# The gated merge's sum and the last scaling of the rows leave VectorE for ScalarE and GpSimd; the queries' high half is cast on ScalarE

## The chip, the cores and the metric

The kernel runs on one core of a Trainium2 chip, from one launch. The metric is the device time of that launch in microseconds. Engines are called as the profile calls them: PE is TensorE (PEld its weight loads), DVE VectorE, ACT ScalarE, POOL GpSimd, and SP the queue that issues nearly all DMAs.

## The reference, cut to what matters

One decoder layer over 2048 rows of 1024 values: a combined projection, sparse attention (branch A), a chunked state-space scan (branch B), a gated merge of the two, an output projection, a residual, and a last RMSNorm. The change touches the parts below:

```
q, k = rope(q), rope(k);  o_a = softmax(top-256 keys) @ v * silu(z_a)
g_a, g_b = split(sigmoid(gates + gate_bias))
merged = g_a * (o_a @ w_branch_a) + g_b * (o_b @ w_branch_b)
x = x + merged @ w_out
out = x * rsqrt(mean(x*x) + eps) * final_norm_w
```

The kernel keeps fp32 accuracy with pairs of fp16 numbers: a value is split into a high half and the rest (low half), and a product takes three matmuls (high x high, high x low, low x high). The gates are stored as tanh(gate/2), so that a sigmoid is (tanh + 1) / 2.

## The kernel before, in words

The rows are worked in 16 tiles of 128. The first 1440 us are projections, the scan and the choice of keys. Then comes the stage that the change is in, to the end. Three streams are interleaved in it, by a rule that spends the estimated time of each in proportion:

- att_A(i) loads the queries of tile i (`q32`), splits them into fp16 halves `q1` (L1387, L1388), has them transposed by a DMA (`Q1`, L1393), and finds each row's largest logit: matmuls `lq` (L1401), each read by DVE (L1404). Its result goes into `q2`, and a second transposing DMA (`Q2`, L1419).
- att_B(i) goes over groups of 4 heads and 128 keys: two matmuls make logits `lg` (L1489, L1491), DVE adds the mask (L1498, tile `p32`), ACT takes the exponential (L1499) and casts it to fp16 `ph` (L1503), POOL makes the low half `pl` (L1506), and PE multiplies both with the values (L1434, L1435, L1444), three groups later. At the end of a tile POOL multiplies with the gate (L1450), and a DMA transposes the result (`oT`, L1351).
- fin_M(i) and fin_O(i) finish tile i in two halves of 512 columns. fin_M loads the gates (`gtl`, L1526, two buffers), makes `pa` (12 matmuls, L1530 to L1532) and `pb` (24, L1537 to L1539) in PSUM, and then on DVE: L1542 (gate + 1) x pa, L1543 (gate + 1) x pb, and L1544 the sum `mg` = first x `f1` + second, where `f1` (`va` in the profile) is one scale per row. ACT squares `mg` and sums it over the row (L1545). After both halves a row scale is made on DVE, ACT makes the fp16 high half (L1345), DVE the rest (L1348, tile `spm`), and a DMA transposes both into `mT` (L1351). fin_O multiplies `mT` with w_out (48 matmuls, L1568 to L1570), adds the residual on DVE (L1573, tile `xr`), squares it on ACT (L1574), makes 1/rms on DVE (L227 to L237), scales `xr` by it and by `final_norm_w` (L1580), and stores it (L1581).

PSUM has two buffers for `pa`, `pb` and fin_O's sums together, two for `lq` and two for `lg`. `p32` has three buffers, `mg`, `spm`, `mT` and `q1` one. fin_M(i+1) and fin_O(i) are interleaved, so that PE has work while the chain from `pb` to `mT` runs.

The order on each engine is not the order of the code: a scheduler with a cost model of its own puts the instructions of each engine into one fixed sequence. An engine runs its sequence in order, so an instruction that waits holds up all that stand behind it.

Of the kernel before, what the change touches and what calls it, by code (L numbers as in the profile page):

```python
# [15 lines left out]
AF = mybir.ActivationFunctionType  # L16
OP = mybir.AluOpType
# [7 lines left out]
NT = S // P  # L25
# [15 lines left out]
def MARK(label):  # L41
    pass
# [115 lines left out]
def hybrid_block(ctx, tc, a, out, dbg=None):  # L158
    nc = tc.nc
    V, A, PL, PE, SP = nc.vector, nc.scalar, nc.gpsimd, nc.tensor, nc.sync  # L160
# [1169 lines left out]
    def fips(shape):  # L1330
        return psF.tile(shape, FT, name="fi2", tag="fi2")
# [33 lines left out]
    def load_mt(i):  # L1365

        mts[i] = at.tile([P, NT, P], BF, name="mkt")
        SP.dma_start_transpose(mts[i][:, 0:i + 1], msk[i, :, 0:(i + 1) * P])

    def att_A(i):  # L1370

        MARK("attA")
        n = (i + 1) * P
        nck = (n + 511) // 512
        q32 = at.tile([P, H, HD], FT, name="q32")
        SP.dma_start(q32.rearrange("p h d -> p (h d)"), qd[i])
        mk = None
        if i >= 2:
            mk = at.tile([P, n if lag == 1 else S], BF, name="mka", bufs=1)
            SP.dma_start(mk[:, :n], msk[i, :, :n])  # L1380
            if lag > 1:
                load_mt(i)
        yield 1.0
        MARK("attA")
        q1 = at.tile([P, H, 2, HD], F16, name="q1", bufs=1)
        q2 = q2t[0]
        V.tensor_copy(q1[:, :, 0], q32)  # L1387
        V.tensor_tensor(q1[:, :, 1], q32, q1[:, :, 0], OP.subtract)  # L1388
        A.copy(q2[:, :, 0:64], q1[:, :, 0])
        yield 0.5  # L1390
        MARK("attA")
        Q1 = ac.tile([P, H, P], F16, name="Q1", bufs=2)
        SP.dma_start_transpose(Q1, q1.rearrange("p h a d -> p (h a d)"))  # L1393
        yield QY
        mxs_ = at.tile([P, H, 4], FT, name="mxs")
        for h in range(H):
            for c in range(nck):
                MARK("attA")
                c0, c1 = c * 512, min(n, c * 512 + 512)
                ps = psQ.tile([P, 512], FT, name="lq", tag="lq" if PQ_ else "lg2")  # L1400
                PE.matmul(ps[:, :c1 - c0], Q1[:, h], KHt[h // 4][:, c0:c1], start=True, stop=True)  # L1401
                jk = pw.tile([P, 512], BF, name="jk", tag="jk", bufs=1)
                if i >= 2:
                    V.tensor_tensor_reduce(jk[:, :c1 - c0], ps[:, :c1 - c0], mk[:, c0:c1], 1.0, -BIG, OP.add, OP.max, mxs_[:, h, c:c + 1])  # L1404
                else:
                    if i == 1:
                        V.tensor_reduce(mxs_[:, h, 1:2], ps[:, 0:P], axis=AX.X, op=OP.max)
                    V.tensor_tensor_reduce(jk[:, :P], ps[:, n - P:n], cmask, 1.0, -BIG, OP.add, OP.max, mxs_[:, h, 0:1])
                yield (c1 - c0) / 2400
        MARK("attA")  # L1410
        rm = at.tile([P, H], FT, name="rm")
        V.tensor_reduce(rm, mxs_[:, :, :(2 if i == 1 else nck)], axis=AX.X, op=OP.max)
        V.tensor_scalar(rm, rm, -(2.0 ** -15), None, OP.mult)
        V.tensor_copy(q2[:, :, 64], rm)
        V.tensor_tensor(q2[:, :, 65], rm, q2[:, :, 64], OP.subtract)
        yield 0.5
        MARK("attA")
        Q2 = ac.tile([P, H, P], F16, name="Q2", bufs=2)
        SP.dma_start_transpose(Q2, q2.rearrange("p h n -> p (h n)"))  # L1419
        st_[i] = (Q1, Q2)  # L1420
        yield 0.5
# [92 lines left out]
    def fin_M(i, fi):  # L1514
        rows = slice(i * P, (i + 1) * P)
        oT, f1 = oTs.pop(i)
        MARK("finM")
        obt = fi.tile([P, 2, KC, P], F16, name="obt", bufs=1)
        SP.dma_start_transpose(obt.rearrange("p a k t -> p (a k) t"), obn[i].rearrange("t a d -> t (a d)"))
        mg = fi.tile([P, D], FT, name="mg", bufs=1)  # L1520
        f2 = fi.tile([P, 2], FT, name="f2m")
        t = fi.tile([P, 2, D], F16, name="spm", bufs=1)
        for nh in range(2):
            cs_ = slice(512 * nh, 512 * nh + 512)
            gt = fi.tile([P, 2, 512], FT, name="gtl")
            SP.dma_start(gt, gd[i].rearrange("p (b n) -> p b n", b=2)[:, :, 512 * nh:512 * nh + 512])  # L1526
            pa = fips([P, 512])
            for k in range(4):
                MARK("finM")
                PE.matmul(pa, oT[:, 0, k], wpa[0][:, k, cs_], start=(k == 0), stop=False)  # L1530
                PE.matmul(pa, oT[:, 0, k], wpa[1][:, k, cs_], start=False, stop=False)
                PE.matmul(pa, oT[:, 1, k], wpa[0][:, k, cs_], start=False, stop=(k == 3))  # L1532
                yield 0.64
            pb = fips([P, 512])
            for k in range(KC):
                MARK("finM")
                PE.matmul(pb, obt[:, 0, k], wpb[0][:, k, cs_], start=(k == 0), stop=False)  # L1537
                PE.matmul(pb, obt[:, 0, k], wpb[1][:, k, cs_], start=False, stop=False)  # L1538
                PE.matmul(pb, obt[:, 1, k], wpb[0][:, k, cs_], start=False, stop=(k == KC - 1))  # L1539
                yield 0.64  # L1540
            MARK("finM")
            V.scalar_tensor_tensor(gt[:, 0], gt[:, 0], 1.0, pa, OP.add, OP.mult)  # L1542
            V.scalar_tensor_tensor(gt[:, 1], gt[:, 1], 1.0, pb, OP.add, OP.mult)  # L1543
            V.scalar_tensor_tensor(mg[:, cs_], gt[:, 0], f1, gt[:, 1], OP.mult, OP.add)  # L1544
            A.activation(t[:, 1, cs_].bitcast(BF), mg[:, cs_], AF.Square, accum_out=f2[:, nh:nh + 1])  # L1545
        V.tensor_tensor(f2[:, 0:1], f2[:, 0:1], f2[:, 1:2], OP.add)
        s_m, v_m = rowscale(f2[:, 0:1], "rm", fi)
        fo = fi.tile([P, 1], FT, name="fo")
        V.tensor_tensor(fo, v_m, io, OP.mult)
        mT = fi.tile([P, 2, KC, P], F16, name="mT", bufs=1)  # L1550
        yield from split_T(mg, s_m, t, mT, KC, i == NT - 1)
        st_[-1 - i] = (mT, fo)

    def fin_O(i, fi):
# [3 lines left out]
        xr = [fi.tile([P, 512], FT, name="xr", bufs=3) for _ in range(2)]  # L1558
# [4 lines left out]
        for nh in range(2):  # L1563
            cs_ = slice(512 * nh, 512 * nh + 512)
# [12 lines left out]
        rs = rsqrt_h(s1[:, 0:1], "fr", fi)  # L1577
        for nh in range(2):
            cs_ = slice(512 * nh, 512 * nh + 512)
            V.scalar_tensor_tensor(xr[nh], xr[nh], rs, fnw[:, cs_], OP.mult, OP.mult)  # L1580
            SP.dma_start(out[rows, cs_], xr[nh])  # L1581
        yield 0.1

# [43 lines left out]
    def early_att():  # L1627
        for i in range(NA):
            yield from att_A(i)
            yield from att_B(i)  # L1630
            flush()
        yield from att_A(NA)
# [13 lines left out]
    fnw = wf.tile([P, D], FT, name="fnw")  # L1646
# [121 lines left out]
```

## Time and profile before

| what | us |
|---|---|
| median of three runs (lowest, highest) | 2208.75 (2206.44, 2212.06) |
| the profiled execution: time / span of its instructions | 2205.71 / 2204.0 |
| PE busy over the span | 2034.3 (92%) |
| DVE busy | 1762.2 (80%) |
| ACT busy | 1131.5 (51%) |
| POOL busy | 833.1 (38%) |
| mean granted clock of PE | 0.974 |

Busy times overlap. PE's busy time comes from modelled ends of pipelined matmuls, so matmuls overlap in it and a wait is a little longer than the idle time shown. A wait is put down to the engine whose event came last.

### The profile page before, as it was taken

The numbers are of one execution on the slowest core, as the hardware profiler recorded it, in microseconds if no ns is written. First come the engines' busy times: TensorE is split into PE (matmuls) and PEld (weight loads), VectorE is DVE, ScalarE is ACT, GpSimd is POOL, SyncE is SP. The second block draws the span as 40 slices with busy tenths as digits, with TensorE's granted clock in tenths as the row PEclk, the third lists the DMA queues.
The fourth block names the chain that finished last, engine by engine and source line by source line (L and its number), as shares of the span: only waits on it lengthen the run. The fifth ranks groups of instructions, "written<-read, shape, count | busy, mean of one in ns | idle before, by whom it ended". The sixth has DMA issues, their size and how long they took to land. (4 is left out here: it accounts for less than half of the span.)

```text
span 2204.0 us, 45401 instructions
## 1 busy us (share of the span) xinstructions
PE 2034.3 (92%) x16625; PEld 1394.0 (63%) x16625; DVE 1762.2 (80%) x4798; ACT 1131.5 (51%) x1973; POOL 833.1 (38%) x1176
## 2 busy tenths in 40 slices
PE   6898999899999999989999899888999999999987
PEld 4656666566767878868877788644444545545543
DVE  8888888888888577888998887467878888887763
ACT  5444453434343167547745731245566666666671
POOL 4433334543435533311102125124454444445550
PEclk9999999999999999999999999999999999999998
DMA  5444422332223332442344435385455343334231
GB/s 155 122 114 108 97 69 81 96 88 63 66 62 89 102 91 80 89 125 90 119 140 132 130 109 180 93 236 124 103 124 112 99 112 93 78 91 97 72 82 46
DMA packets 371202, 229.19 MB, mean 104 GB/s; under 512 B 209996, under 2 KB 333720, under 8 KB 370968
## 3 DMA queue, kind: packets, MB, share of 16 engines
q1 hardware_dynamic: 370968, 226.19, 38.2%
q8 instruction: 132, 2.16, 0.4%
q14 instruction: 102, 0.84, 0.1%
HBM read 123.82 MB, written 53.90 MB: 81 GB/s over the span
## 5 line engine op out<-in xcount | busy, mean ns | idle before, releaser
L1506 POOL TENSOR_TENSOR pl<-p,ph 128x512 f16<-128x512 f32 x272 | 324.9, 1197 | 427.5 <-ACT ph L1503 426.8
L1499 ACT ACTIVATE p<-p,lnb,qsc 128x512 f32<-128x512 f32 x270 | 217.8, 811 | 216.6 <-DVE p L1498 215.7
L444 PEld LDWEIGHTS <-xh 128*128 128x128 f16 x2560 | 252.5, 100 | 50.1 <-DMA xh<-th 10.7
L445 PEld LDWEIGHTS <-xh 128*128 128x128 f16 x2560 | 251.3, 99 | 38.4 <-issue 3.2
L446 PEld LDWEIGHTS <-xl 128*128 128x128 f16 x2560 | 251.0, 99 | 34.5 <-issue 3.3
L1498 DVE TENSOR_TENSOR p<-lg,mkt 128x512 f32<-128x512 f32 x266 | 181.7, 685 | 68.7 <-PE lg L1491 61.0
L1404 DVE CUSTOM_DVE_ANT_0 jk<-lq,mka 128x512 bf16<-128x512 f32 (+3 forms) x304 | 187.9, 618 | 33.0 <-PE lq L1401 24.4
L1503 ACT CAST ph<-p 128x512 f16<-128x512 f32 x272 | 166.1, 615 | 6.5
L1090 ACT ACTIVATE jkS<-sca,XX 128x384 int8<-128x384 f32 (+3 forms) x104 | 138.6, 1333 | 54.0 <-DVE XX L1080 35.3
L1401 PE MATMUL lq<-KK,Q 128*128 128x512 f16 (+3 forms) x320 | 100.1, 347 | 19.2 <-DVE mxs L1404 14.3
L1491 PE MATMUL lg<-Q,KK 128*128 128x512 f16 x272 | 103.2, 382 | 12.1 <-DMA Q<-q2t 12.0
L1092 DVE TENSOR_SCALAR_CACHE_REDUCE jkV<-sca,XX 128x1536 uint8<-128x1536 f32 (+4 forms) x78 | 111.9, 1434 | 2.6
L1568 PE MATMUL fi<-wo,mT 128*128 128x512 f16 x256 | 98.5, 385 | 15.8 <-DMA mT<-spm 11.1
L1169 ACT ACTIVATE gt<-gt 128x512 f32<-128x512 f32 x64 | 40.1, 627 | 139.8 <-DVE gt L1168 139.4
L1434 PE MATMUL po<-Vt,ph 128*128 128x65 f16 x1088 | 106.4, 193 | 2.4 <-ACT ph L1503 2.1
L954 ACT ACTIVATE r<-acc 128x512 f32<-128x512 f32 (+3 forms) x152 | 79.6, 542 | 55.7 <-DVE sca L955 37.3
L1489 PE MATMUL lg<-Q,KK 128*128 128x512 f16 x272 | 103.8, 382 | 4.0 <-DVE p L1498 3.9
L1435 PE MATMUL po<-Vt,ph 128*128 128x64 f16 x1088 | 106.9, 195 | 0.0
L1444 PEld LDWEIGHTS <-pl 128*128 128x128 f16 x1088 | 65.2, 98 | 57.7 <-issue 5.7
L738 ACT ACTIVATE sj<-zu 128x256 bf16<-128x256 f32 x64 | 26.6, 415 | 145.6 <-POOL zu L736 145.6
L1537 PE MATMUL fi<-wpb,obt 128*128 128x512 f16 x256 | 97.3, 380 | 3.1 <-DVE gtl L1542 2.8
L1569 PE MATMUL fi<-wo,mT 128*128 128x512 f16 x256 | 98.1, 383 | 0.0
(804 smaller groups left out, 6648.1 us busy)
## 6 DMA issues: line engine op xcount, KB each, us to landing
bc<-acr SPq DMA_DIRECT2D x64, 256.0 KB, 3.2
gd<-gt SPq DMA_DIRECT2D x64, 256.0 KB, 2.5
gtl<-gd SPq DMA_DIRECT2D x32, 512.0 KB, 4.0
xt<-in_x SPq DMA_DIRECT2D x16, 512.0 KB, 4.3
e<-ecr SPq DMA_DIRECT2D x128, 64.0 KB, 3.1
obn<-ohl SPq DMA_DIRECT2D x64, 128.0 KB, 2.2
pst<-in_w_out SPq DMA_DIRECT2D x16, 512.0 KB, 4.4
xr<-in_x SPq DMA_DIRECT2D x32, 256.0 KB, 3.1
```

The costliest lines, as they stand in the source:

```text
L444: PE.matmul(ps, xh[:, c, tk], hi[:, c], start=(first and c == 0), stop=False)
L445: PE.matmul(ps, xh[:, c, tk], lo[:, c], start=False, stop=False)
L446: PE.matmul(ps, xl[:, c, tk], hi[:, c], start=False, stop=(last and c == KC - 1))
L1090: A.activation(jkA[:, :n], sct[i], AF.Sign, bias=thr[:, 0, k:k + 1], scale=-1.0, accum_out=cnt[:, 0, k:k + 1])
L1092: V.tensor_scalar(jkV[:, :n], sct[i], thr[:, 0, k:k + 1], 0.0, OP.is_lt, OP.add, accum_out=cnt[:, 0, k:k + 1])
L1404: V.tensor_tensor_reduce(jk[:, :c1 - c0], ps[:, :c1 - c0], mk[:, c0:c1], 1.0, -BIG, OP.add, OP.max, mxs_[:, h, c:c + 1])
L1434: PE.matmul(B["po"][:, h, 0:65], ph[:, h], Vt[:, j, g, 0:65], start=(j == 0 and h == 0), stop=False)
L1435: PE.matmul(B["po"][:, h, 0:64], ph[:, h], Vt[:, j, g, 65:129], start=False, stop=False)
L1498: V.tensor_tensor(p32, ps, mb, OP.add)
L1499: A.activation(p32, p32 if masked and not onP else ps, AF.Exp, bias=lnb, scale=qsc[g])
L1503: A.copy(ph, p32)
L1506: PL.tensor_tensor(pl, p32, ph, OP.subtract)
```

## The change

Four edits, all in the last stage. The code of the last tile (i = 15) keeps the old form of the second, third and fourth.

1. The cast of the queries to their high half goes from DVE to ACT.
2. After the gate's load, ACT makes (gate A + 1) x f1 in place (an activation Identity with a per-row scale and bias), so that DVE's first product is a plain one.
3. The sum `mg` goes from DVE to POOL, as an addition of two fp32 tiles in SBUF.
4. The last scaling goes from one DVE instruction to two: ACT multiplies by the row's 1/rms, POOL by `final_norm_w`.

```
-        V.tensor_copy(q1[:, :, 0], q32)
+        A.copy(q1[:, :, 0], q32)
...
             SP.dma_start(gt, gd[i].rearrange("p (b n) -> p b n", b=2)[:, :, 512 * nh:512 * nh + 512])
+            if i < NT - 1:
+                A.activation(gt[:, 0], gt[:, 0], AF.Identity, bias=f1, scale=f1)
...
-            V.scalar_tensor_tensor(gt[:, 0], gt[:, 0], 1.0, pa, OP.add, OP.mult)
-            V.scalar_tensor_tensor(gt[:, 1], gt[:, 1], 1.0, pb, OP.add, OP.mult)
-            V.scalar_tensor_tensor(mg[:, cs_], gt[:, 0], f1, gt[:, 1], OP.mult, OP.add)
+            if i < NT - 1:
+                V.tensor_tensor(gt[:, 0], gt[:, 0], pa, OP.mult)
+                V.scalar_tensor_tensor(gt[:, 1], gt[:, 1], 1.0, pb, OP.add, OP.mult)
+                PL.tensor_tensor(mg[:, cs_], gt[:, 0], gt[:, 1], OP.add)
+            else:
+                V.scalar_tensor_tensor(gt[:, 0], gt[:, 0], 1.0, pa, OP.add, OP.mult)
+                V.scalar_tensor_tensor(gt[:, 1], gt[:, 1], 1.0, pb, OP.add, OP.mult)
+                V.scalar_tensor_tensor(mg[:, cs_], gt[:, 0], f1, gt[:, 1], OP.mult, OP.add)
...
-            V.scalar_tensor_tensor(xr[nh], xr[nh], rs, fnw[:, cs_], OP.mult, OP.mult)
+            if i < NT - 1:
+                A.activation(xr[nh], xr[nh], AF.Copy, scale=rs)
+                PL.tensor_tensor(xr[nh], xr[nh], fnw[:, cs_], OP.mult)
+            else:
+                V.scalar_tensor_tensor(xr[nh], xr[nh], rs, fnw[:, cs_], OP.mult, OP.mult)
             SP.dma_start(out[rows, cs_], xr[nh])
```

The scheduler makes new sequences from it. In what the kernel runs on these inputs, PE has the same instructions, and of its 31,449 rows most keep their order; SP's DMAs change places in seven spots. Lines after L1526 have other numbers in the changed kernel: L1528 is the new activation, L1546 the product with `pb`, L1547 POOL's sum, L1552 the square, L1589 POOL's scaling.

DVE at the second half of tile 6's merge, before:

```order
L1498 TENSOR_TENSOR p_22862<-lg_22859,mkt 128x512
L1387 CAST q_23840<-q_23728 128x8x64
L1388 TENSOR_TENSOR q_23840<-q_23728,q_23840 128x8x64
L1543 SCALAR_TENSOR_TENSOR gtl<-gtl,fi_22723 128x512
L1544 SCALAR_TENSOR_TENSOR mg<-gtl,va 128x512
L1498 TENSOR_TENSOR p_22899<-lg_22896,mkt 128x512
L1498 TENSOR_TENSOR p_22938<-lg_22935,mkt 128x512
L1546 TENSOR_TENSOR f2m<-f2m 128x1
```

And DVE at the same place in the changed kernel:

```order
L1498 TENSOR_TENSOR p_22886<-lg_22883,mkt 128x512
L1388 TENSOR_TENSOR q_23871<-q_23756,q_23871 128x8x64
L1546 SCALAR_TENSOR_TENSOR gtl<-gtl,fi_22747 128x512
L1498 TENSOR_TENSOR p_22923<-lg_22920,mkt 128x512
L1553 TENSOR_TENSOR f2m<-f2m 128x1
L1498 TENSOR_TENSOR p_22962<-lg_22959,mkt 128x512
L1338 TENSOR_SCALAR rmt<-f2m 128x1
```

The cast and the sum are gone from between the mask additions, and the sum over the row (`f2m`), which needs ACT's square, stands one mask addition earlier.

POOL near there before (`oa` is the attention's output of the tile):

```order
L1506 TENSOR_TENSOR pl<-p_22831,ph 128x512
L1506 TENSOR_TENSOR pl<-p_22862,ph 128x512
L1450 TENSOR_TENSOR oa<-oa,za 128x256
L1506 TENSOR_TENSOR pl<-p_22899,ph 128x512
L1506 TENSOR_TENSOR pl<-p_22938,ph 128x512
```

And POOL there in the changed kernel, up to the scaling of the tile before:

```order
L1506 TENSOR_TENSOR pl<-p_22886,ph 128x512
L1547 TENSOR_TENSOR mg<-gtl 128x512
L1506 TENSOR_TENSOR pl<-p_22923,ph 128x512
L1450 TENSOR_TENSOR oa<-oa,za 128x256
L1506 TENSOR_TENSOR pl<-p_22962,ph 128x512
L1506 TENSOR_TENSOR pl<-p_23016,ph 128x512
L1506 TENSOR_TENSOR pl<-p_23045,ph 128x512
L1506 TENSOR_TENSOR pl<-p_23108,ph 128x512
L1506 TENSOR_TENSOR pl<-p_23140,ph 128x512
L1589 TENSOR_TENSOR xr<-xr,fnw 128x512 x2
L1506 TENSOR_TENSOR pl<-p_23187,ph 128x512
```

The sum stands right behind the `pl` of the last group whose cast ACT has issued before it squares the sum; both scalings of a tile stand together between two `pl`.

ACT at this place before (`spm,f2m` is the square with its sum, L1545):

```order
L1499 ACTIVATE p_22862<-p_22862,lnb,qsc_9034 128x512
L1503 CAST ph<-p_22862 128x512
L1545 ACTIVATE spm,f2m<-mg 128x512
L1499 ACTIVATE p_22899<-p_22899,lnb,qsc_9034 128x512
L1499 ACTIVATE p_22938<-p_22938,lnb,qsc_9034 128x512
L1503 CAST ph<-p_22899 128x512
L1345 ACTIVATE spm<-mg,rms 128x1024
```

And ACT there in the changed kernel:

```order
L1387 CAST q_23871<-q_23756 128x8x64
L1499 ACTIVATE p_22886<-p_22886,lnb,qsc_9034 128x512
L1503 CAST ph<-p_22886 128x512
L1552 ACTIVATE spm,f2m<-mg 128x512
L1499 ACTIVATE p_22923<-p_22923,lnb,qsc_9034 128x512
L1503 CAST ph<-p_22923 128x512
L1345 ACTIVATE spm<-mg,rms 128x1024
```

The square (L1552) follows the cast `ph<-p_22886`, whose `pl` POOL does ahead of the sum: nothing else of ACT lies between them.

## Rows read from the trace of the kernel before

**Rows 1.** Stretch view: us, busy us of each engine (instructions), PE clock, DMA share, GB/s.

```profile
1450.00:2150.00 700.00, 651.26 (x5652) 343.88 (x5651) 563.83 (x1435) 437.39 (x702) 329.64 (x289) 0.99 0.43 105
```

**Rows 2.** Waits, 1450 to 2150 us: who for whom, us in total, times, longest.

```profile
ACT spm L1545 <- DVE mg L1544: 18.5, 11, 7.3
...
PE lq L1401 <- DVE mxs L1404: 13.2, 21, 1.5
...
PE fi L1568 <- DMA mT<-spm: 11.1, 6, 2.5
PE lg L1491 <- DMA Q<-q2t: 8.8, 5, 2.6
...
PE lg L1489 <- DVE p L1498: 3.9, 5, 1.3
PE fi L1568 <- DVE gtl L1542: 3.6, 2, 2.7
...
PE fi L1537 <- DVE gtl L1542: 2.8, 1, 2.8
```

**Rows 3.** Groups, DVE, 1450 to 2150 us: count | busy us, mean ns | idle before.

```profile
L1348 DVE SCALAR_TENSOR_TENSOR spm<-mg,rms,spm 128x512 f16<-128x512 f32 x30 | 32.7, 1128 | 5.7 <-ACT spm L1345 5.7
L1580 DVE SCALAR_TENSOR_TENSOR xr<-xr,fry,fnw 128x512 f32<-128x512 f32 x27 | 27.0, 1038 | 0.1
L1544 DVE SCALAR_TENSOR_TENSOR mg<-gtl,va 128x512 f32<-128x512 f32 x29 | 25.4, 875 | 0.2
...
L1387 DVE CAST q<-q 128x512 f16<-128x512 f32 x12 | 7.4, 616 | 8.6 <-DMA Q<-q 5.0 <-DMA q<-qd 2.6 <-ACT p L1499 0.9
```

**Rows 4.** Groups, POOL and ACT, the same stretch.

```profile
L1506 POOL TENSOR_TENSOR pl<-p,ph 128x512 f16<-128x512 f32 x262 | 313.0, 1197 | 352.7 <-ACT ph L1503 352.2
L1499 ACT ACTIVATE p<-p,lnb,qsc 128x512 f32<-128x512 f32 x261 | 210.7, 811 | 204.3 <-DVE p L1498 203.4
...
L1503 ACT CAST ph<-p 128x512 f16<-128x512 f32 x261 | 159.5, 615 | 6.4
...
L1450 POOL TENSOR_TENSOR oa<-oa,za 128x256 f32<-128x256 f32 x27 | 20.3, 752 | 18.6 <-DVE oa L1449 15.9 <-DVE rms L1339 2.4
...
L1345 ACT ACTIVATE spa<-oa,ras 128x512 f16<-128x512 f32 x13 | 9.3, 712 | 0.6 <-DVE ras L1339 0.6
```

**Rows 5.** Timeline, DVE near 1614 us: start, us, engine, line.

```profile
1613.00 1.41 DVE L1580 SCALAR_TENSOR_TENSOR xr<-xr,fry,fnw 128x512 f32<-128x512 f32 x2
...
1615.06 0.69 DVE L1404 CUSTOM_DVE_ANT_0 jk<-lq,mka 128x512 bf16<-128x512 f32 x1
```

**Rows 6.** Timeline, PE at the same time.

```profile
1613.68 0.38 PE L1401 MATMUL lq<-KK,Q 128*128 128x512 f16 x1
1613.90 0.38 PE L1489 MATMUL lg<-Q,KK 128*128 128x512 f16 x1
1615.81 0.22 PE L1401 MATMUL lq<-KK,Q 128*128 128x128 f16 x1 [1.53 <-DVE mxs L1404]
```

**Rows 7.** Tile mg: shortest/median/longest duration in ns.

```profile
L1544 DVE SCALAR_TENSOR_TENSOR mg<-gtl,va x32: 722/751/1609, 1440.8 to 2175.7; 128x512 f32<-128x512 f32 x32
...
L1348 DVE SCALAR_TENSOR_TENSOR spm<-mg,rms,spm x32: 735/766/1655, 1460.1 to 2179.7; 128x512 f16<-128x512 f32 x32
```

**Rows 8.** Timeline, DVE and POOL near 1774 us.

```profile
1773.69 1.16 POOL L1506 TENSOR_TENSOR pl<-p,ph 128x512 f16<-128x512 f32 x1 [2.02 <-ACT ph L1503]
...
1773.79 1.61 DVE L1544 SCALAR_TENSOR_TENSOR mg<-gtl,va 128x512 f32<-128x512 f32 x1
```

**Rows 9.** Timeline, DVE, ACT and POOL at the merge of tile 6, second half.

```profile
1744.88 1.16 POOL L1506 TENSOR_TENSOR pl<-p,ph 128x512 f16<-128x512 f32 x1 [0.92 <-ACT ph L1503]
...
1745.60 0.99 DVE L1544 SCALAR_TENSOR_TENSOR mg<-gtl,va 128x512 f32<-128x512 f32 x1
...
1746.62 0.63 ACT L1545 ACTIVATE spm<-mg 128x512 bf16<-128x512 f32 x1 [1.88 <-DVE mg L1544]
```

**Rows 10.** Tile gtl: the load's time from issue to landing.

```profile
DMA to landing us min/median/max: 3.9/4.0/5.7
```

## Prediction

> **What bounds the kernel now.** I read the stretch view first, for the only stage that the change touches: of the 700 us from 1450 to 2150, DVE is busy 563.8 (81%), ACT 437.4 (62%), POOL 329.6 (47%), and PE shows 651.3 at a granted clock of 0.99 [rows 1]. PE is the engine that sets the pace, with DVE close behind it. So I asked the waits next, for what PE itself waits for [rows 2]. Two sorts matter. DVE ends 13.2 + 3.9 + 3.6 + 2.8 = 23.5 us of PE's idle time in 29 waits, most of them of the `lq` matmul, whose two PSUM buffers DVE must read first. Transposing DMAs end 11.1 + 8.8 = 19.9 us in 11 waits, `mT` and `Q2`. The idle time understates a wait: at 1613.90 PE issues a matmul, at 1615.81 the next, 1.91 us where matmuls follow each other by 0.22 us (1613.68 to 1613.90), so 1.69 us are lost where the row says 1.53 [rows 6]. With 0.16 us more for each wait, DVE costs PE 23.5 + 29 x 0.16 = 28.1 us, and the DMAs 19.9 + 11 x 0.16 = 21.7 us. Nothing that the change does can win more than part of these 50 us; the rest of the stage is matmuls.
>
> Why DVE is late can be seen at that same wait: the two scalings of L1580 held DVE for 1.41 us from 1613.00, and only at 1615.06 did it come to the `lq` result for which PE was waiting [rows 5]. DVE is fast enough on average; it is late after bursts, and the sums, the scalings and the fp16 remainders make the bursts.
>
> **DVE: what is removed.** In this stage 27 of L1580, 29 of L1544 and 12 of L1387 are shown [rows 3], and all of them go (the last tile's keep their place, but run after 2150). That is 27.0 + 25.4 + 7.4 = 59.8 us, so DVE falls from 563.8 to about 504 us, 72%. The first product loses its added constant and keeps its length. What of the 59.8 reaches PE is bounded by 0 (the bursts that remain suffice for every wait) and by all 28.1 us. I take half, 14 us: about a quarter of DVE's bursts goes, and the time that DVE needs to work off a burst shrinks faster than its load, since its idle share grows from 19% to 28%. Nothing is gained from the wait ahead of L1387 (8.6 us, mostly for DMAs [rows 3]): L1388 now waits at the same place for ACT's cast, which waits for the same DMAs.
>
> **ACT: what is added.** 30 activations with a per-row scale and bias, at L1499's 811 ns (it has both); 30 scaled copies, at L1345's 712 ns; 12 casts, at L1503's 615 ns [rows 4]: 24.3 + 21.4 + 7.4 = 53.1 us, which makes ACT 490 us, 70%. This lies beside ACT's idle time, most of which is waiting for DVE's mask additions (203.4 us [rows 4]). The new activation also waits for the gates' load. That load is issued when POOL's sum has freed the buffer, which is when ACT may start the square, and lands 4.0 us later [rows 10]. In the first halves of the later tiles one or two exponentials stand between, so ACT gets there after some 0.8 + 0.8 + 0.6 = 2.2 us and is held up to 1.8 us. Behind it wait the exponentials, for which PE has three groups of cover. I take 1 us for it all; 0 to 6 would be the bounds (15 waits of 1.8 us are 27 us of ACT, of which I let a fifth through).
>
> **POOL: what is added.** 30 sums and 30 products of 128 x 512 fp32 values with both inputs in SBUF. The nearest row has 1197 ns for this size with an fp16 output; 752 ns for half the size in fp32 bounds it from above with 1504 [rows 4]. At 1197 it is 71.8 us, and POOL goes to 401 us, 57%. POOL's own idle time covers that (it waits 352.2 us for `ph` [rows 4]). What it costs lies in two other places.
>
> The first is the path from `pb` to `mT`, on which the sum lies. A sum takes 1197 ns in place of DVE's mean of 875, 0.3 us more, and stands behind one `pl`. In tile 6 POOL is busy with that until 1744.88 + 1.16 = 1746.04; a sum would then end at 1747.24 and the square start 0.6 us later than its 1746.62 [rows 9]. Against that, where DVE had other work between the second product and the sum, POOL is earlier, and the chain's later steps on DVE find it less busy. I take 0.4 us for each chain; PE waited for `mT` 6 times by its matmuls, some 8 tiles have no slack to speak of, so 8 x 0.4 = 3 us. Bounds: 4 us won (0.5 us earlier each) and 15 x 1.5 = 22 us lost.
>
> The second is that DVE and POOL block each other. L1544 usually takes 751 ns, but 1609 at 1773.79, just after POOL began a `pl` of 1.16 us [rows 7, 8]; L1348 has a mean of 1128 and a shortest of 735, so 30 x 0.39 = 11.8 us of its time are waiting [rows 3, 7]. With POOL busy 57% in place of 47% that becomes a fifth more, 2.5 us of DVE time; priced like the removed work (14 / 59.8) it is 0.6 us. The removed instructions were blocked too, and their means include it. The Trainium skill (SBUF — State Buffer, "Who interferes with whom") gives this as a rule: an instruction of VectorE with two SBUF inputs and one of GpSimd that reads SBUF share a port pair, and the one that starts second is blocked for the whole of the other. By that rule, the trace agrees: the longest L1544 is its shortest plus 0.89 us, most of a `pl`. It speaks against giving GpSimd more to do, and with every one of the 30 L1348 blocked for a whole `pl` DVE would lose 30 x (1.2 - 0.39) = 24 us more, which at the same price changes the sum by 5.7 us.
>
> SP is held longer by the output rows, which now wait for ACT's copies and POOL's products (about 0.7 x 2 + 1.2 x 2 = 3.8 us in place of 1.4). Behind them in its queue stand the loads of the next `xr`, whose buffers they free, and then a gate load that has to wait for the next sum anyway; I cost it at nothing, and up to 2 us a tile where `Q2` or `oT` stands close behind.
>
> **The sum.** -14 + 1 + 3 + 0.6 = -9.4 us. On the profiled execution (2205.7) that is 2196.3. The median of the runs is 3.0 us above that execution, so the median should come to 2199.
>
> **Rivals.** *The waits change hands.* PE gains on `lq` and arrives sooner at `mT` and `Q2`, whose transposes take as long as before. For: 21.7 us of PE's waits are for DMAs already, and the tiles that wait for `mT` have no slack, so what PE wins between `pb` and `mT` it loses there. Against: the DVE waits are spread over the tile, and that path is perhaps a third of it; `Q2` also depends on DVE's maxima, which come sooner. It would leave some 4 us: about 2205.
>
> *GpSimd's queue is the new late one; slower.* The sum waits behind a `pl`, which waits for ACT's cast, and ACT has nothing to do between that cast and the square. If the chain to `mT` is 1.5 us longer in each of the 15 tiles, it is 22 us; the scalings, two together, 2.4 us, hold back `pl` and the product before `oT` as well, which DVE's next row scale waits for. With 3 us for that and 14 us won on DVE the kernel is some 11 us slower, about 2220. It decides from about 0.9 us per tile on. For: ACT already lost 18.5 us waiting for the sum [rows 2]. Against: tile 6 shows 0.6 us, and POOL stands idle more than half of the time.
>
> *DVE's waits go altogether.* With all 28.1 us gone and the costs above (28 - 4.6 = 23.5 us), 2185. For: at 72% a queue is seldom long. Against: L1348's pairs, often over 2 us, stay.
>
> That the change is without effect can be left out: the order of the instructions shows what has moved.
>
> **How the numbers follow.** Chances: the forecast 0.50 (its own range 2190 to 2202), DVE's waits gone 0.10, hands changed 0.24, GpSimd late 0.16. About 0.3% (6.6 us) is what a measurement of this kernel can tell from no change. Forecast and third rival are faster by more than that: 0.60; the first rival is within it: 0.24; the second is slower: 0.16. The range from 2186 to 2216 leaves out a little of the best and of the worst case.
>
> **What the profile after would show.** In the corresponding 700 us DVE is busy about 505 us; `lq`'s waits for DVE fall from 13.2 to 5 to 8 us; POOL's sums and products take about 1.2 us; ACT's wait for the sum, now POOL's, is no longer than 25 us; PE's waits for `mT` are 11 to 16 us. I am wrong if PE's waits for DVE stay near 23 us (the bursts that remain are the cause), or if the waits for `mT` or for `ph` grow by as much as DVE's shrink.

## The result, and the profile after

The changed kernel takes 2224.32 us (median of 6 runs, 2221.59 to 2230.59) where the kernel before takes 2209.99 (6 runs on the same chip, 2206.01 to 2212.06). The ratio is 1.0074, with a 95% interval of 1.0058 to 1.0089: slower by 0.74%, some 16 us on 2210. (Ratios are estimated from the single runs, so they are not quite the quotients of the medians, which lie 14.3 us apart here.) The forecast was 2199 us and faster; 2224 lies outside its range.

The profiled execution of after took 2230.59 us, the longest of its six, and its first sum `mg` already starts 6.8 us later than that of before (1447.6 against 1440.8 [rows 7]), in a part of the program that the change hardly touches (three of edit 1's sixteen casts lie there); over all the profiles below that start varies from 1440.8 to 1453.4. So I compare the stage alone, from the first start of an instruction that makes `mg` to the last. In before that is 1440.8 to 2175.7, 734.9 us [rows 7]. In after it is 1447.6 to 2199.5, 751.9 us, in the rows of the tile `mg` (shortest/median/longest duration in ns, first and last start):

```profile
L1547 POOL TENSOR_TENSOR mg<-gtl x30: 1270/1297/1732, 1447.6 to 2162.2; 128x512 f32<-128x512 f32 x30
...
L1551 DVE SCALAR_TENSOR_TENSOR mg<-gtl,va x2: 752/752/752, 2191.7 to 2199.5; 128x512 f32<-128x512 f32 x2
```

The stage is 17.0 us longer, which is the whole loss by the ratio. The stretch view of the stage, before and then after (columns as in [rows 1]), shows in what form:

```profile
1440.80:2175.70 734.90, 684.17 (x5834) 359.51 (x5833) 576.17 (x1454) 447.22 (x721) 337.98 (x294) 0.99 0.43 105
1447.60:2199.50 751.90, 687.93 (x5834) 360.45 (x5833) 521.13 (x1384) 488.38 (x791) 404.58 (x352) 0.98 0.43 103
```

PE has the same 5834 matmuls in both. Its busy time grew by 3.8 us, at a mean granted clock of 0.98 where it was 0.99. Its idle time, the rest of the stage, grew by 13.2 us, from 50.7 to 64.0. So the lower clock can account for no more than these 3.8 us of the 17.0; the rest is waiting.

The same view for 700 us of after, beside [rows 1], shows that the relief of DVE itself came as worked out:

```profile
1450.00:2150.00 700.00, 640.61 (x5476) 336.09 (x5475) 501.58 (x1340) 463.89 (x750) 384.79 (x336) 0.98 0.44 106
```

DVE went from 563.8 to 501.6 us. But in the same 700 us PE finished 5476 matmuls where it had finished 5652 [rows 1]. The waits of after, 1450 to 2175 us (who for whom, us in total, times, longest), say who was late:

```profile
ACT spm L1552 <- POOL mg L1547: 51.7, 26, 3.2
...
ACT gtl L1528 <- DMA gtl<-gd: 24.3, 16, 3.5
DVE f2m L1553 <- ACT spm L1552: 21.0, 14, 2.8
PE lq L1401 <- DVE mxs L1404: 17.3, 17, 2.1
DVE q L1388 <- ACT q L1387: 16.6, 8, 4.6
...
PE lg L1491 <- DMA Q<-q2t: 10.4, 7, 2.8
PE fi L1575 <- DVE gtl L1545: 9.8, 5, 3.3
...
PE fi L1575 <- DMA mT<-spm: 7.3, 3, 3.3
...
PE po L1434 <- ACT ph L1503: 4.6, 7, 1.0
PE fi L1539 <- DVE gtl L1545: 4.5, 2, 3.8
...
PE lg L1489 <- DVE rmt L1338: 3.0, 4, 1.4
```

PE's four largest waits for DVE are 17.3 + 9.8 + 4.5 + 3.0 = 34.6 us, where they were 23.5 [rows 2], although DVE has less to do. The rows of DVE and ACT above them say why: DVE stands still for 21.0 us at the f2 sum, because ACT's square is not done, and for 16.6 us at L1388, because ACT's cast is not done. ACT in turn stands still for 51.7 us at the square, because GpSimd's sum is not done; in before that wait was 18.5 us and for DVE [rows 2]. PE's waits for DMAs are no larger: 10.4 + 7.3 = 17.7 us against 19.9.

One case in full, from the timeline of after near 1770 us (start, us, engine, line; in brackets the idle time before and what ended it):

```profile
1767.78 0.62 ACT L1503 CAST ph<-p 128x512 f16<-128x512 f32 x1
...
1768.28 0.69 DVE L1498 TENSOR_TENSOR p<-lg,mkt 128x512 f32<-128x512 f32 x1
...
1768.54 1.17 POOL L1506 TENSOR_TENSOR pl<-p,ph 128x512 f16<-128x512 f32 x1 [1.61 <-ACT ph L1503]
...
1769.66 1.28 POOL L1547 TENSOR_TENSOR mg<-gtl 128x512 f32<-128x512 f32 x1
...
1770.97 0.63 ACT L1552 ACTIVATE spm<-mg 128x512 bf16<-128x512 f32 x1 [2.57 <-POOL mg L1547]
...
1771.60 0.80 ACT L1499 ACTIVATE p<-p,lnb,qsc 128x512 f32<-128x512 f32 x1
...
1771.73 0.16 DVE L1553 TENSOR_TENSOR f2m<-f2m 128x1 f32<-128x1 f32 x1 [2.75 <-ACT spm L1552]
1771.81 0.69 DVE L1498 TENSOR_TENSOR p<-lg,mkt 128x512 f32<-128x512 f32 x1
1771.83 0.38 PE L1577 MATMUL fi<-wo,mT 128*128 128x512 f16 x1
...
1772.43 0.62 ACT L1503 CAST ph<-p 128x512 f16<-128x512 f32 x1
...
1772.55 0.38 PE L1489 MATMUL lg<-Q,KK 128*128 128x512 f16 x1 [0.35 <-DVE rmt L1338]
...
1773.19 1.16 POOL L1506 TENSOR_TENSOR pl<-p,ph 128x512 f16<-128x512 f32 x1 [2.25 <-ACT ph L1503]
```

The sum waits in GpSimd's queue for a `pl`, which waits for ACT's `ph`. ACT, next in its own queue, has the square and stands for 2.57 us; DVE, next in its queue, has the f2 sum and stands for 2.75 us. Behind the square stands the exponential of the next group, although DVE had finished its mask addition at 1768.97; behind the f2 sum stands the mask addition of 1771.81. That addition ends at 1772.50 and gives PE its `lg` bank back, so the `lg` matmul starts at 1772.55 (the row names `rmt`, which DVE runs next), 0.72 us after the matmul before it where 0.22 is usual. And GpSimd, whose sum had started all this, then stands idle for 2.25 us, since ACT's cast is late. Three engines wait in a ring for one instruction of 1.28 us.

### The profile page after: what moved, and what is told of

It reads as the page before. It is cut to its first block, busy times and chain, and to the rows that moved or that the text cites. A ratio compares the mean times of both kernels' runs of the same rounds, so it can differ in the third digit from the quotient of the medians.

```text
span 2228.9 us, 45543 instructions
## 1 busy us (share of the span) xinstructions
PE 2041.1 (92%) x16625; PEld 1397.2 (63%) x16625; DVE 1705.7 (77%) x4722; ACT 1176.8 (53%) x2049; POOL 900.9 (40%) x1236
## 4 chain that ended last, share of the span: by engine, by line
PE 44%; DVE 25%; DMA 9%; issue 8%; ACT 8%; POOL 6%; SPq 1%; DVEq 0%; POOLq 0%; ACTq 0%
PE acc L444 5%; PE acc L446 5%; PE acc L445 5%; DVE cac L551 3%; PE lq L1401 2%; DVE bc L701 2%; PE fi L1539 2%; PE fi L1540 2%; PE fi L1541 2%; PE lg L1491 2%; PE lg L1489 2%; PE fi L1575 2%; PE fi L1577 2%; PE fi L1576 2%; DMA Q<-q2t 1%
## 5 line engine op out<-in xcount | busy, mean ns | idle before, releaser
L1506 POOL TENSOR_TENSOR pl<-p,ph 128x512 f16<-128x512 f32 x272 | 318.5, 1176 | 343.0 <-ACT ph L1503 342.7
L446 PEld LDWEIGHTS <-xl 128*128 128x128 f16 x2560 | 250.9, 99 | 34.6 <-issue 3.9
L1575 PE MATMUL fi<-wo,mT 128*128 128x512 f16 x256 | 98.2, 384 | 18.2 <-DVE gtl L1545 9.8
L1539 PE MATMUL fi<-wpb,obt 128*128 128x512 f16 x256 | 98.3, 384 | 4.7 <-DVE gtl L1545 4.5
L1540 PE MATMUL fi<-wpb,obt 128*128 128x512 f16 x256 | 98.4, 384 | 0.0
```

The costliest lines, as they stand in the source:

```text
L446: PE.matmul(ps, xl[:, c, tk], hi[:, c], start=False, stop=(last and c == KC - 1))
L1506: PL.tensor_tensor(pl, p32, ph, OP.subtract)
```

## The experiments

Theory A: the loss is these waits, the sum's above all, at the head of queues that run in order. Rival B: the loss is GpSimd's load as such. Rival C: it is the new order of the instructions alone, no edit being to blame. The fourth column is the stage in one profiled execution, measured as above (before 734.9, changed kernel 751.9).

| kernel | median us / before on the same chip | ratio (95% interval) | stage us |
|---|---|---|---|
| e1: edit 1 | 2216.63 / 2216.31 | 1.0011 (0.9993 to 1.0029) | 737.2 |
| e2: edit 2, sum on DVE | 2218.44 / 2216.31 | 1.0009 (0.9989 to 1.0030) | 738.9 |
| e23: edits 2, 3 | 2223.59 / 2216.31 | 1.0028 (1.0012 to 1.0044) | 746.7 |
| e4: edit 4 | 2214.15 / 2216.31 | 0.9995 (0.9978 to 1.0013) | 736.9 |
| e123: without edit 4 | 2222.07 / 2209.59 | 1.0060 (1.0041 to 1.0080) | 747.7 |
| e234: without edit 1 | 2216.39 / 2209.59 | 1.0036 (1.0024 to 1.0049) | 740.3 |
| b_y: order alone | 2215.11 / 2215.75 | 0.9993 (0.9979 to 1.0007) | 736.8 |
| b_less: relief alone | 2189.39 / 2209.59 | 0.9916 (0.9897 to 0.9936) | 718.4 |
| x_junk: load, no wait | 2221.32 / 2215.75 | 1.0022 (1.0005 to 1.0039) | 745.8 |
| x_pass: load and wait | 2221.27 / 2209.59 | 1.0062 (1.0042 to 1.0081) | 742.2 |
| x_twice: the sum twice | 2256.15 / 2215.75 | 1.0178 (1.0160 to 1.0196) | 771.1 |
| x_id: edit 2 later | 2231.71 / 2215.75 | 1.0055 (1.0033 to 1.0076) | 753.6 |
| x_free: all, sum not waited for | 2208.53 / 2210.57 | 0.9985 (0.9970 to 1.0001) | 734.7 |
| x_free1: the same without edit 1 | 2201.94 / 2210.57 | 0.9955 (0.9933 to 0.9977) | 731.2 |
| h: half of the sum, one square | 2206.96 / 2210.57 | 0.9979 (0.9964 to 0.9995) | 734.3 |
| h4: h and edit 4 | 2203.92 / 2209.25 | 0.9978 (0.9965 to 0.9992) | 727.9 |
| b_sq1: one square alone | 2207.02 / 2209.25 | 0.9987 (0.9970 to 1.0004) | 731.9 |
| e4r: edit 4 in other order | 2210.14 / 2210.57 | 1.0009 (0.9991 to 1.0027) | 734.9 |

0.1% is 2.2 us. Ratios are compared below, since the medians of before differ by up to 7 us between the groups of runs. The stage column is a single execution of each kernel and shares in its scatter.

**The edits one by one.**

```
e1   q1 cast:  -V.tensor_copy(...)  +A.copy(...)
e2   +A.activation(gt[:, 0], gt[:, 0], AF.Identity, bias=f1, scale=f1)
     +V.tensor_tensor(mg[:, cs_], gt[:, 0], gt[:, 1], OP.add)
e23  the same, with PL.tensor_tensor(mg[:, cs_], gt[:, 0], gt[:, 1], OP.add)
e4   +A.activation(xr[nh], xr[nh], AF.Copy, scale=rs)
     +PL.tensor_tensor(xr[nh], xr[nh], fnw[:, cs_], OP.mult)
```

> Edit 1 alone: the fp16 cast of the queries on ACT, all else as before. Theory A (ACT's queue is held, and DVE's subtraction behind the cast then waits for ACT: 8 waits, 16.6 us, in the trace of the changed kernel against none before): 2 to 5 us slower than before, about 2213 us. Rival B (the loss is the sum's longer way through GpSimd): no loss here, 2206 to 2210 us, since DVE is relieved of some 9 us. Rival C (the loss is in how the changed work falls into TensorE's order and its half-clock stretches, with no edit to blame): any value within 5 us of before, and the single edits would not add up to the 14 us of the whole.

> Edit 2 alone: ACT prepares f1 times (gate A plus 1) behind the gate's load, DVE multiplies it by the product and still makes the sum (as a plain sum). Theory A: the new ACT instruction waits for the gate's transfer (16 waits, 24.3 us, in the changed kernel) and holds what stands behind it on ACT; DVE's work is about as before: 3 to 6 us slower, about 2214 us. Rival B: no change, 2208 to 2212 us. Rival C: within 5 us of before on either side.

> Edits 2 and 3: as edit 2 alone, with the sum on GpSimd. Theory A: ACT's square of the sum waits for GpSimd (26 waits, 51.7 us, in the changed kernel, against 11 waits, 18.5 us, for DVE before) and DVE's f2 sum behind it: 6 to 11 us slower than before, about 2219 us. Rival B: nearly the whole loss, 11 to 15 us slower, with the waits of the normed rows' transfer (mT) grown in the trace. Rival C: within 5 us of before.

> Edit 4 alone: the last scaling as an ACT copy with a scale and a GpSimd product. Nothing on the path to the next tile waits for its result. Theory A: ACT holds 28 further instructions of 0.71 us that start only when DVE's row scale is there, so other ACT work waits up to that long, and DVE is relieved of 34 us: the two about cancel, 2206 to 2212 us. Rival B: a gain, 2200 to 2207 us, as the loss is all in edit 3. Rival C: within 5 us of before.

Only e23 differs from before by more than its interval, 0.28%; e1, e2 and e4 can't be told from no change. The new wait of ACT for the gate's load is there in e2 (16 times, 21.7 us between 1450 and 2165) and costs next to nothing. The four ratios add up to 0.11 + 0.28 - 0.05 = 0.34%, less than half of 0.74%. The edits seem to cost more together than apart; by the four intervals the difference of 0.40% is only just clear of zero (0.07 to 0.73). So:

> The changed kernel without edit 4 (the last scaling back on DVE). If the edits' costs add up (e1 and e23: 2.4 and 6.2 us), some 9 us slower than before; theory A with ACT's queue as the shared resource: edit 4 puts 28 more ACT instructions into that queue, so leaving it out takes 3 to 6 us off the changed kernel, again 8 to 12 us slower than before.

> The changed kernel without edit 1 (the cast of the queries back on DVE). If the edits' costs add up, 5 us slower than before; theory A: DVE's wait for the cast (16.6 us) goes, 3 to 5 us off the changed kernel, 9 to 12 us slower than before.

Leaving out edit 4 gains 0.14%, which the intervals cover; leaving out edit 1 gains 0.38%, 8 us (4 to 13 by the two intervals), where edit 1 alone cost 2 with an interval around zero. That it costs more in company is likely and not certain: the intervals allow a difference from 0 to 12 us. The waits of e234 (1450 to 2165 us), where the cast is on DVE again:

```profile
ACT spm L1552 <- POOL mg L1547: 50.7, 25, 3.3
...
DVE f2m L1553 <- ACT spm L1552: 20.4, 14, 3.0
```

The sum's waits are as in the full change, and L1388's wait for ACT is gone. In e1 that wait was 10.0 us in 5 times, in the full change 16.6 in 8. I read this as ACT, held at the square, reaching the cast late, so that DVE, held at the f2 sum, is then held again; x_free below bears on it.

**Order alone.** One more place to interleave between the sum and the f2 sum:

```
+        yield 0.64
         V.tensor_tensor(f2[:, 0:1], f2[:, 0:1], f2[:, 1:2], OP.add)
```

> A control of order alone: the kernel before with one more place (0.64 in the interleaver's units) between the second sum and the f2 sum, at which it may put work of the other streams; no instruction is added, removed or moved to another engine. Theory A: within 3 us of before. Rival C: such a shift of order alone moves the time by 5 us or more to either side, and then the differences of the single edits are no larger than that.

No change. This is one shift of order among many that are possible, but it gives no sign that order alone moves the time by 16 us.

**The relief alone.** Third product and last scaling left out in tiles 0 to 14:

```
-            V.scalar_tensor_tensor(gt[:, 1], gt[:, 1], 1.0, pb, OP.add, OP.mult)
-            V.scalar_tensor_tensor(mg[:, cs_], gt[:, 0], f1, gt[:, 1], OP.mult, OP.add)
+            V.scalar_tensor_tensor(mg[:, cs_], gt[:, 1], 1.0, pb, OP.add, OP.mult)
...
-            V.scalar_tensor_tensor(xr[nh], xr[nh], rs, fnw[:, cs_], OP.mult, OP.mult)
```

> The kernel before with 56 of DVE's instructions left out in tiles 0 to 14: the sum mg (mg gets the second product alone, the first is not added) and the last scaling (the rows go out unscaled). DVE is relieved of some 60 us, and no other engine gets any of it: the relief term of the prediction by itself. Theory A (the relief is worth what the prediction said, and the new waits ate it): 8 to 14 us faster than before, PE's waits for DVE fall by half. Rival D (the relief is worth little, since PE waits for DVE through chains of single instructions and not for its load): 0 to 4 us faster.

0.84% faster, 18.6 us, more than either theory expected. The waits of b_less, 1450 to 2135 us:

```profile
PE lq L1401 <- DVE mxs L1404: 8.5, 9, 1.8
...
PE fi L1572 <- DMA mT<-spm: 6.2, 4, 2.7
```

`lq`'s wait falls from 13.2 [rows 2] to 8.5 us, and `mT`'s from 11.1 to 6.2. Without the sum the chain from `pb` to `mT` is also an instruction shorter, and the runs don't divide this from the load. The lower wait for `mT` doesn't prove the shorter chain at work, since it fell as far where the chain is as long as before or longer (5.2 us in b_y's stage, 7.3 in the changed kernel). Rival D's 0 to 4 us are refuted for the two together; for the load alone they are not.

**The wait on the sum.** x_junk and x_pass give GpSimd the same 30 additions. In x_junk nobody uses them; in x_pass they make `mg`:

```
x_junk  V.scalar_tensor_tensor(mg[:, cs_], gt[:, 0], f1, gt[:, 1], OP.mult, OP.add)
       +PL.tensor_tensor(gt[:, 0], gt[:, 0], gt[:, 1], OP.add)
x_pass +V.scalar_tensor_tensor(gt[:, 0], gt[:, 0], f1, gt[:, 1], OP.mult, OP.add)
       +PL.tensor_tensor(mg[:, cs_], gt[:, 0], gt[:, 1], OP.add)
```

> The kernel before, with one GpSimd addition per column half behind DVE's sum: the same two gate tiles, the same 128 x 512 fp32 size, its result used by nobody. GpSimd thus gets the sum's work and the gate tile is held as long as in the changed kernel, but ACT and DVE wait for DVE's sum as before. Theory A (what costs is that ACT's square and DVE's f2 sum wait for GpSimd's late sum): within 4 us of before. Rival B (what costs is GpSimd's load itself: its queue, its share of the SBUF port): 6 to 8 us slower, the step from e2 to e23.

> The kernel before with DVE's sum kept (into the gate tile) and a GpSimd addition of the same tiles behind it that makes mg (the second product is in it twice). It has the instructions of x_junk; the difference is that ACT's square and DVE's f2 sum wait for GpSimd's result. Theory A: 6 to 12 us slower than x_junk, 11 to 17 us slower than before, with DVE's waits for ACT's square at 20 us or more. Rival B (GpSimd's load is the cost): as x_junk, 5 us slower than before.

x_junk is 0.22% slower, x_pass 0.62%. The intervals just fail to touch: the additions without the wait cost something (5 us, with 1 to 9 in the interval), the wait on top of it some 9 (3 to 15). The profiles are of no help here, since in the one execution of each x_junk's stage is the longer one (745.8 against 742.2 us). The waits of x_pass (1450 to 2165 us):

```profile
ACT spm L1549 <- POOL mg L1546: 56.5, 27, 9.3
...
DVE f2m L1550 <- ACT spm L1549: 14.3, 13, 1.9
```

DVE's wait is 14.3 us, not the 20 or more that I expected. Nor is x_junk load alone. Its addition stands right behind DVE's sum, and in 12 of 15 tiles DVE's small f2 sum (128 x 1) starts while it runs and ends with it. The f2 sum's rows of before and x_junk (shortest/median/longest in ns), and one case from x_junk's timeline:

```profile
L1546 DVE TENSOR_TENSOR f2m<-f2m x16: 144/156/619, 1457.3 to 2177.2; 128x1 f32<-128x1 f32 x16
L1548 DVE TENSOR_TENSOR f2m<-f2m x16: 147/452/1226, 1468.5 to 2197.5; 128x1 f32<-128x1 f32 x16
...
2022.13 1.28 POOL L1546 TENSOR_TENSOR gtl<-gtl 128x512 f32<-128x512 f32 x1
...
2022.21 1.22 DVE L1548 TENSOR_TENSOR f2m<-f2m 128x1 f32<-128x1 f32 x1
```

So some of x_junk's 5 us is the f2 sum held up in another way, and the pair understates the wait if anything. It leaned to A without settling it. The dose and the removal did. The dose:

```
                 PL.tensor_tensor(mg[:, cs_], gt[:, 0], gt[:, 1], OP.add)
+                PL.tensor_tensor(mg[:, cs_], gt[:, 0], gt[:, 1], OP.add)
```

> The changed kernel with GpSimd's sum made twice, one right behind the other, with the same result: a dose of 1.29 us per column half on the wait in question, nothing on DVE or ACT. Theory A: ACT's waits for the sum grow from 51.7 to some 80 us, DVE's for the square from 21 to some 38 us, and the time goes up by 8 to 18 us over the changed kernel, 22 to 32 us over before. Rival B: some 7 us over the changed kernel. Rival C (order and half-clock stretches alone): within 5 us of the changed kernel.

1.78% over before, so 1.0% or 23 us over the changed kernel, where A had allowed 8 to 18, for 30 x 1.28 = 38 us of GpSimd's time. Its waits, 1450 to 2195 us:

```profile
ACT spm L1553 <- POOL mg L1548: 77.2, 28, 4.0
...
DVE f2m L1554 <- ACT spm L1553: 32.3, 13, 3.7
...
PE po L1434 <- ACT ph L1503: 11.5, 8, 2.5
```

ACT's wait grows by 25.5 us and DVE's by 11.3, and PE's wait for `ph` rises from 4.6 to 11.5, as ACT's casts stand behind the square. PE's wait for `mT` does not grow (6.2 us against 7.3). The removal, with the same instructions on every engine:

```
-                V.scalar_tensor_tensor(gt[:, 1], gt[:, 1], 1.0, pb, OP.add, OP.mult)
-                PL.tensor_tensor(mg[:, cs_], gt[:, 0], gt[:, 1], OP.add)
+                V.scalar_tensor_tensor(mg[:, cs_], gt[:, 1], 1.0, pb, OP.add, OP.mult)
+                PL.tensor_tensor(gt[:, 0], gt[:, 0], gt[:, 1], OP.add)
```

> The changed kernel with the same instructions on every engine, but nobody waits for GpSimd's sum: DVE's second product goes into mg itself, GpSimd adds the two gate halves into the gate tile, and that result is used by nobody (so the first product is missing from the output). Theory A: the wait's price goes, 9 to 14 us faster than the changed kernel, 2 to 7 us slower than before. Rival (the load on ACT and GpSimd, or the order, is the price): within 4 us of the changed kernel, 12 us or more slower than before.

> As x_free, without edit 1 (the cast of the queries back on DVE), so neither the sum nor the cast is waited for. Theory A: another 3 to 8 us faster than x_free, 5 us faster than before to no change. Rival (edit 1's price in company is ACT's load in general): as x_free.

x_free: 0.15% faster than before, with no change just inside its interval, so 0.89% or 20 us faster than the changed kernel (15 to 25 by the two intervals); more than A said. x_free1: another 0.30% (7 us, an interval of about 1 to 13), and 0.45% faster than before. Against e234, which has no edit 1 either, it is 0.81% or 18 us faster: the removal gives about the same a second time. The waits of x_free, 1450 to 2155 us:

```profile
ACT gtl L1528 <- DMA gtl<-gd: 24.9, 19, 2.8
...
PE lq L1401 <- DVE mxs L1404: 12.5, 13, 2.6
...
PE fi L1575 <- DMA mT<-spm: 9.3, 6, 3.0
...
DVE q L1388 <- ACT q L1387: 8.2, 6, 2.4
...
PE fi L1575 <- DVE gtl L1545: 6.5, 3, 3.3
...
ACT spm L1552 <- DVE mg L1546: 1.6, 4, 0.6
...
DVE f2m L1553 <- ACT spm L1552: 1.4, 4, 0.8
```

The f2 sum's wait goes from 21.0 to 1.4 us, the wait for the cast from 16.6 to 8.2 though nothing was done to the cast, and `lq`'s from 17.3 to 12.5. The halved wait for the cast fits the reading above. But edit 1 costs as much here (7 us) as in the full change (8 us), so what its price hangs on stays open.

The stage of x_free in the stretch view:

```profile
1445.20:2179.90 734.70, 687.12 (x5839) 360.79 (x5838) 526.43 (x1385) 492.28 (x792) 401.49 (x351) 0.98 0.44 105
```

PE is busy as long as in the changed kernel (687.1 us against 687.9), at the same clock; its idle time is 47.6 us where it was 64.0. The 17 us of the stage are thus waits of PE. The wait for the gate's load is what it was (24.9 us). x_free also takes the sum out of the chain to `mT`; PE's wait for `mT` is no shorter for it (9.3 us against 7.3), so I put the 20 us down to the queues; the load (rival B) is the same in both. That the shorter chain has no part in it is argued from this wait alone: no run takes away the waits and keeps the sum in the chain.

**The gate's wait.** The preparation written behind `pa`'s matmuls:

```
-            if i < NT - 1:
-                A.activation(gt[:, 0], gt[:, 0], AF.Identity, bias=f1, scale=f1)
             pa = fips([P, 512])
...
+            if i < NT - 1:
+                A.activation(gt[:, 0], gt[:, 0], AF.Identity, bias=f1, scale=f1)
             pb = fips([P, 512])
```

> The changed kernel with ACT's preparation of the gate written behind the first product's matmuls (pa) instead of right behind the gate's load. The gate's transfer should then be in before ACT comes to it: the wait of 16 times and 24.3 us goes below 8 us. Theory A: 2 to 6 us faster than the changed kernel, 8 to 12 us slower than before. Rival (the gate's wait was ACT's idle time anyway, only the sum on GpSimd counts): within 2 us of the changed kernel, 14 us slower than before.

The edit missed: the scheduler put the instruction nearly where it had been, and the wait for the load stayed (32.7 us between 1400 and 2190, where the changed kernel shows 32.0 from 1406 to 2201). The 0.55% agrees with the changed kernel's 0.74% within the intervals. On the gate's wait it says nothing; e2 does.

**Is there a version without the waits?** h sums the first column half on GpSimd and the second on DVE, and squares both at once:

```
+                (V if nh else PL).tensor_tensor(mg[:, cs_], gt[:, 0], gt[:, 1], OP.add)
...
-            A.activation(t[:, 1, cs_].bitcast(BF), mg[:, cs_], AF.Square, accum_out=f2[:, nh:nh + 1])
-        V.tensor_tensor(f2[:, 0:1], f2[:, 0:1], f2[:, 1:2], OP.add)
+        A.activation(t[:, 1].bitcast(BF), mg, AF.Square, accum_out=f2[:, 0:1])
```

> Edits 2 and 3 with the sum on GpSimd for the first column half alone (DVE sums the second), and one ACT square over both halves behind the second sum in place of one for each half; the result is complete. GpSimd's sum is done long before the square, so nobody waits for it. Theory A: within 3 us of before, where e23 was 6.2 us slower. Rival (GpSimd's load): 2 to 4 us slower.

0.21% faster than before, 4.6 us, and the square no longer waits for GpSimd at all (1450 to 2155 us):

```profile
PE lq L1401 <- DVE mxs L1404: 9.7, 15, 1.2
...
ACT spm L1552 <- DVE mg L1547: 6.0, 6, 3.1
```

How much of it is the single square, b_sq1 asks (the last three lines of that diff on the kernel before); h4 adds edit 4 to h; and e4r turns the steps of edit 4 round, the product on GpSimd behind the square, the scaling on ACT last.

> The kernel before with one ACT square over the whole row in place of one for each column half, and so without DVE's f2 sum; nothing else changes. If h's gain is that of the sum's half on GpSimd, this is within 2 us of before; if it is the single square's, 3 to 5 us faster, as h. The square's longer single step could also cost on the way to the transposed rows: up to 4 us slower.

> h with edit 4 added (the last scaling on ACT and GpSimd); the result is complete. In x_free1, where nobody waited for the sum or the cast, the three edits 2 to 4 gave 10 us. Theory A: 4 to 9 us faster than before, so 0 to 4 us faster than h. Rival (edit 4 takes what it gives, as e4 and e4r say): as h, 3 to 5 us faster than before.

> Edit 4 with its two steps in the other order: GpSimd multiplies by final_norm_w right behind the square, while the row sum is made, and ACT scales by the row's 1/rms last. In e4 GpSimd waited for ACT's copy (8 times, 14.8 us) with the probabilities' low parts queued behind it; here it doesn't. Theory A: 2 to 6 us faster than before. Rival (the load on GpSimd and ACT takes the relief, not a wait): as e4, within 2 us of before.

b_sq1: 0.13%, between no change and h; the gain of h can't be divided with these intervals. h4: 0.22%, as h. e4r: no gain, as e4; GpSimd now waits for ACT's square (15.1 us in 11 times) where it had waited for ACT's copy (14.8 us in 8). Edit 4 changed nothing that can be measured in three places (alone, in e234 against e23, in h4 against h), with 17 to 21 us less busy time on DVE in the stage each time. Whether its relief is lost to a wait or was worth nothing in the first place stays open: leaving out the scaling alone wasn't tried. The fastest versions that leave nothing out are h and h4, 0.2% faster than before.

## Why the prediction was wrong

**DVE's relief, -14 us.** Right in load (about 504 us forecast, 501.6 measured). Whether that load is worth 14 us is not shown: b_less, which leaves out 60 of the 72 instructions (its expectation says 56, a miscount), gave 18.6 us, but with a shorter chain to `mT` too, and edit 4, with its share of the relief, gained nothing in any of the three places above. What the relief needed, and what the working never asked, was whether DVE can use its time. In after, DVE's new waits for ACT are 21.0 + 16.6 = 37.6 us in this stage.

**The sum on GpSimd, +3 us.** This is the step that failed. It priced the later sum at "0.4 us for each chain" on the one path from `pb` to `mT`, and took PE's waits for `mT` as the place where it would show. That place didn't get worse: 11.1 us before [rows 2], 7.3 after. (Over the stage this wait lies between 5.2 and 11.8 us in all twenty profiles, so 20 us can't hide there.) The price was paid by what stands behind the two instructions that wait for the sum: exponentials and `ph` casts behind ACT's square, mask additions and `lq` maxima behind DVE's f2 sum. Measured: 20 us (15 to 25), x_free against the changed kernel. The forecast's own signs show it: ACT's wait for the sum was to be no longer than 25 us and is 51.7, and `lq`'s was to fall to 5 to 8 us and is 17.3. In the place of "how much later does the chain end" the question was "which queues stop while the sum is late". The text had the piece in hand, that the sum stands behind a `pl` which waits for ACT, and used it only for the rival's 1.5 us on the `mT` chain. That rival, "GpSimd's queue is the new late one; slower", had the sign, about the size (2220) and the culprit, with a chance of 0.16, but its path was wrong too. The argument against it, GpSimd idle more than half of the time, failed as well: an idle engine delays others when its next instruction waits.

**ACT, +1 us, and the cast at nothing.** The gate's wait came as described (16 times, 24.3 us) and was rightly cheap: e2 is 0.09% slower with an interval around zero. "L1388 now waits at the same place for ACT's cast, which waits for the same DMAs" was wrong. L1387's wait in before was 8.6 us, mostly for DMAs [rows 3]; L1388 now waits 16.6 us, and ACT's own wait for those DMAs at the cast is only 5.9 us, by its row in the groups of after (1450 to 2175 us):

```profile
L1387 ACT CAST q<-q 128x512 f16<-128x512 f32 x13 | 8.0, 615 | 5.9 <-DMA q<-qd 3.8 <-DMA Q<-q 2.0
```

The rest is that ACT gets there late. Alone the edit is not to be told from nothing, in company it costs 8 us (e234).

**The shared port, +0.6 us.** The changed kernel shows no sign of the growth that I gave it. L1348, the instruction that showed it before [rows 3, 7], in the groups of after, 1450 to 2175 us:

```profile
L1348 DVE SCALAR_TENSOR_TENSOR spm<-mg,rms,spm 128x512 f16<-128x512 f32 x30 | 27.1, 943 | 4.8 <-ACT spm L1345 4.8
```

Its mean fell from 1128 to 943 ns with GpSimd busier. GpSimd's share is thus no measure of how often the two block each other. Where the blocking does show is x_junk, on another instruction: the f2 sum, two inputs in SBUF, took up to 1226 ns where 156 is its median before. The rule of the Trainium skill (SBUF — State Buffer, "Who interferes with whom") is that a VectorE instruction with two SBUF inputs and a GpSimd one that reads SBUF contend for a shared port pair, which the first to start holds to its end. The trace of x_junk agrees: the f2 sum of 2022.21 ends 0.02 us after the addition that it met. So the rule tells what happens when two instructions meet; its price in the prediction rested on their meeting more often, which the changed kernel's rows don't show.

With the waits on the sum and the cast gone, x_free1 is 10 us faster than before, by its interval 5 to 15. That this is near the forecast's -9.4 is partly luck: x_free1 has a shorter chain to `mT` and leaves the cast on DVE, and its parts don't fit term by term (18.6 us for most of the relief, 5 us for additions that nobody uses). What is shown is the difference: two waits that were priced at 3 us and at nothing cost some 26 (x_free1 against the changed kernel, 1.19%).

## What to carry to other kernels

When an instruction moves to another engine, list who waits for its result, and for each of them what stands behind it in its in-order queue: the price can be paid there, while the chain that ends at the next tile shows nothing. Work can move to a slower engine without loss when its result is needed late (the first half's sum in h), and moves badly when two engines have its consumers next in their queues. The prices of single edits need not add up (0.34% apart, 0.74% together here), so the whole has to be measured, and parts taken out of it.

## What the runs showed that I had not expected

A GpSimd addition of two 128 x 512 fp32 tiles took 1297 ns (median of 30), 12% more than the 1158 ns of `pl` with its fp16 output (median, in the rows of the tile `pl` of after), where I had taken them as equal; the product with `final_norm_w` took 1274 ns (mean, in the groups of after, 1450 to 2175 us). The two rows:

```profile
L1506 POOL TENSOR_TENSOR pl<-p,ph x272: 1146/1158/1681, 1401.5 to 2174.3; 128x512 f16<-128x512 f32 x136
```

```profile
L1589 POOL TENSOR_TENSOR xr<-xr,fnw 128x512 f32<-128x512 f32 x26 | 32.6, 1274 | 16.2 <-ACT xr L1588 16.2
```

And an extra delay on the sum costs most of itself: 38 us of additions made x_twice 23 us slower than the changed kernel, while some 36 us of GpSimd products that no other engine waits for (e4) left the time where it was, though there DVE was relieved of 20 us as well.
